# Adding the seven Strassen sums to the residual in separate steps, and one output-gate group of 512 columns instead of two of 256

## The chip, the cores and the metric

The kernel runs on 1 core of one Trainium2 chip. The metric is the device time of one execution in microseconds (us). A core has a matrix engine, TensorE (PE in the profile, its weight loads PEld), a vector engine, VectorE (DVE), a scalar engine, ScalarE (ACT), GpSimd (POOL) and SyncE (SP), which here issues the weight transfers. Each engine works through its own list of instructions in order and waits on the others by semaphores.

## The reference

Two encoder layers on `x` of 256 tokens by 2048 channels in float32. The first layer mixes tokens by pooling and attention, the second by a bidirectional matrix memory (mLSTM) with 8 heads of 256. After each mixer comes a gated MLP with a width-3 convolution. Cut to what the change touches:

```
# second layer's mixer, after the scans gave h_fw + h_bw
o_gate = sigmoid(proj[..., 3*W:4*W])
hn = hsum * rsqrt(mean(hsum*hsum) + eps) * h_norm      # per head
y = (hn * o_gate) @ w_out
# gated MLP (both layers), D_FF = 5632
u = conv3(rms_norm(x) @ w_up) ; gate, val = split(u)
x = x + (silu(gate) * val) @ w_down
```

## The kernel before, in words

**Matmuls in three terms.** Every float32 product is computed as high times high, high times low and low times high part. A weight chunk (128 x 1024) is loaded by SyncE (L100), ACT casts it to its high part (L120), DVE subtracts that to get the low part (L121): "a split". `Stream` (L79) keeps loads five and splits two chunks ahead; four split buffers `hl` rotate, so a cast waits until PE has finished the chunk four before.

**Woven tasks.** `Weave` (L145) holds generators. After each k tile of a matmul group, `tick` lets virtual time advance and runs at most one task that is due; so small pieces of work are placed between matmuls. PE's order is as written. The orders of ACT, DVE and SP are set by a scheduler that plays the program through on a modelled timeline, except where `keep_in_program_order` fixes an instruction.

**The MLP** (`ffn_layer`, L911). The 44 tiles of the inner width come in chunks of 4, 8, 8, 8, 8, 8 (`FCH`). For each tile, `up` (L929) runs 64 + 64 matmuls, then a chain on DVE and ACT: gather (L400, L401), scale (L933), convolution (L938 to L942), SiLU (L946), product (L947), high part of `g` (L948, ACT), low part (L949, DVE). The output's left 1024 columns are computed by `down` (L1043) chunk by chunk. The right 1024 columns of the first five chunks are computed with seven products instead of eight (Strassen in Winograd's form): `unit` (L973) runs products and adds them chunk by chunk into `acc`, seven tiles of 128x512 (L998, L1000). When the fifth chunk's products are complete, `total` (L1004) adds the sums of `acc` to `x`: two operations within `acc` (L1008, L1009) and nine on `x` (L1013). It is called while the last tile's chain is still on the way; then the sixth and last chunk goes through `down` for all four 512-column blocks `b`, as tiles `dn` (in the second layer the last block as `end`, L1015). `residual` (L407, adding at L410) adds a finished block to `x`. In the first layer, `nxt.add(b)` then squares the block and weaves in its transposes (`xt`, L288), whose results are scaled into `xx` (L300, L303) for the next layer.

**The mixer of the second layer** (`mlstm_layer`, L701) handles head pairs `hp` = 0 to 3: values `mv`, queries and keys `mq` and `mk`, and output gates `mo`. `mov_group` (L375) runs a group with the activations as stationary operand: 6 matmuls per k tile, of `width` columns. For `hp` 0 to 2 the pair's gates are one group of 512 columns, for the last pair two groups of 256 (L899 to L903). `gated` (L848) then takes exp (L851), adds one (L855), takes reciprocals in place (L857), multiplies the head (L861), transposes it (`htr`, L866) and writes it to `mcat` (L870, L871). `out_proj` (L412) first multiplies heads 0 to 5 for blocks 0 and 1, waits by `ready` for heads 6 and 7, and goes on with them.

The order of the weights on the host (`_ml_chunks`, L1111) follows that of the groups.

Of the kernel before, what the change touches and what calls it, by code (L numbers as in the profile page):

```python
# [190 lines left out]
def trunk(ctx: ExitStack, tc: tile.TileContext, gx, xT, xn, call, catt, cml, weights, out):  # L191
# [167 lines left out]
    def mov_part(ps, act, kts, first, last):  # L359

        n = len(kts)
        hl = None
        for i, k in enumerate(kts):
            if i % 2 == 0:
                hl = st.next()
            src, c = act(k), i % 2 * 512
            wh, wl = hl[:, 0, c : c + 512], hl[:, 1, c : c + 512]
            for t in range(2):
                xh, xl = (src[:, j, t * P : t * P + P] for j in range(2))
                mm(ps[:, t], xh, wh, first and i == 0, False)  # L370
                mm(ps[:, t], xh, wl, False, False)
                mm(ps[:, t], xl, wh, False, last and i == n - 1)
            wv.tick(1.29)
# [33 lines left out]
    def residual(ps, b, eng=None):  # L407
        for t in range(2):
            xs = x[:, t, b * 512 : b * 512 + 512]
            v.tensor_add(xs, xs, ps[:, t])  # L410
# [290 lines left out]
    def mlstm_layer(norm, nxt):  # L701
        with ExitStack() as es:
# [145 lines left out]
            def gated(ps, heads):  # L848
                og = t1p.tile([P, 2, len(heads) * MD], F32, tag="og", name=f"og{heads[0]}")
                for t in range(2):  # L850
                    a.activation(og[:, t, :], ps[:, t, :], AF.Exp, scale=nrcol[:, t : t + 1])  # L851
                yield 1.2
                for i, h in enumerate(heads):
                    o = og[:, :, i * MD : i * MD + MD]
                    v.tensor_scalar_add(o, o, 1.0)  # L855
                    for t in range(2):
                        tc.keep_in_program_order(v.reciprocal(o[:, t], o[:, t]))  # L857
                        yield 2.5
                    yield from wv.wait(lambda: h in hns)
                    hn = hns[h]  # L860
                    tc.keep_in_program_order(v.tensor_mul(hn, hn, o))  # L861
                    yield 4.5
                    tr = psp.tile([P, 2, S], F32, tag="ps", name=f"htr{h}")
                    for e in range(2):
                        for t in range(2):
                            pe.transpose(tr[:, e, t * P : t * P + P], hn[:, t, e * P : e * P + P], ident)  # L866
                    for e in range(2):
                        c = cat(2 * h + e)
                        gn = cst[:, C_HN + 2 * h + e : C_HN + 2 * h + e + 1]
                        a.activation(c[:, 0, :], tr[:, e, :], AF.Copy, scale=gn)  # L870
                        v.scalar_tensor_tensor(c[:, 1, :], tr[:, e, :], gn, c[:, 0, :].bitcast(F32),  # L871
                                               ALU.mult, ALU.subtract)
                    done.add(h)
# [3 lines left out]
            for hp in range(MH // 2):  # L877
                vf = t1p.tile([P, 2, 512], F32, tag="vf", name=f"mvf{hp}")
                for c, n in ((0, MD + 32), (MD, MD)) if hp == 0 else ((0, 512),):
                    ps = mov_group(xx, f"mv{hp}_{c}", n)  # L880
                    if hp + c == 0:
                        wv.until(lambda: norm.rcol is not None)
                        wv.add(gates(ps))
                    n = min(n, 512 if hp else MD)
                    for t in range(2):
                        a.activation(vf[:, t, c : c + n], ps[:, t, :n], AF.Copy, scale=norm.rcol[:, t : t + 1])
                vt = t1p.tile([P, 2, 2, 512], F32R, tag="vt", name=f"mvt{hp}")
                a.copy(vt[:, 0], vf)
                v.tensor_sub(vt[:, 1], vf, vt[:, 0].bitcast(F32))
                if hp == 0:  # L890
                    nrcol = kp.tile([P, 2], F32, tag="nrcol", name="nrcol")
                    v.tensor_scalar_mul(nrcol, norm.rcol, -1.0)
                for hh in range(2):
                    h = 2 * hp + hh
                    q = scaled(stat_group(xx, list(range(KT)), f"mq{h}"), f"q{h}", MD ** -0.5)
                    kk = scaled(stat_group(xx, list(range(KT)), f"mk{h}"), f"k{h}", 1.0)
                    wv.add(head(h, q, kk, vt, hh))
                heads = [2 * hp, 2 * hp + 1]
                if hp < MH // 2 - 1:  # L899
                    wv.add(gated(mov_group(xx, f"mo{hp}"), heads))  # L900
                else:
                    for h in heads:
                        wv.add(gated(mov_group(xx, f"mo{hp}_{h}", MD), [h]))  # L903

            def ready(i):
                wv.until(lambda: set(range(6 + 2 * i)) <= done)
# [4 lines left out]
    def ffn_layer(layer, norm, nxt):  # L911
        with ExitStack() as es:
# [60 lines left out]
            def unit(kind, c, j):  # L973

                n = FCH[c] // 2
                order = (4, 6, 5, 3) if kind == "A" else (0, 1, 2)
                if j == 0:
                    for e in order:
                        pss[e] = psp.tile([P, 512], F32, tag="ps", name=f"pp{layer}_{c}_{e}")
                gt = gts[c]  # L980
                s3, s1 = combos[c, j]

                def part(k, t):
                    return [gt[:, 2 * j + k, i, t * P : t * P + P] for i in range(2)]

                if kind == "A":
                    xs = [[s3[:, i, m] for i in range(2)] for m in (1, 0, 2)] + [part(1, 1)]
                else:
                    xs = [part(0, 0), part(1, 0), [s1[:, i] for i in range(2)]]
                for m, e in enumerate(order):  # L990
                    if m % 2 == 0:
                        hl = st.next()
                    wh, wl = (hl[:, i, m % 2 * 512 : m % 2 * 512 + 512] for i in range(2))
                    product(pss[e], xs[m], wh, wl, j == 0, j == n - 1)
                if j == n - 1:
                    for e in order:
                        if c == 0:
                            a.copy(acc[:, e], pss[e])  # L998
                        else:
                            v.tensor_add(acc[:, e], acc[:, e], pss[e])  # L1000
                    if kind == "B" and c == len(FCH) - 2:
                        total()

            def total():  # L1004

                p1, p2, p3, q4, p5, q6, p7 = (acc[:, e] for e in range(7))
                x00, x01, x10, x11 = (x[:, t, c : c + 512] for t in range(2) for c in (1024, 1536))
                v.tensor_sub(q6, q6, p1)  # L1008
                v.tensor_sub(p5, q6, p5)  # L1009
                for xs, op, e in ((x01, v.tensor_add, p5), (x01, v.tensor_sub, p3), (x11, v.tensor_add, p5),  # L1010
                                  (x11, v.tensor_sub, p7), (x10, v.tensor_sub, q6), (x10, v.tensor_add, p7),
                                  (x10, v.tensor_add, q4), (x00, v.tensor_add, p1), (x00, v.tensor_add, p2)):
                    op(xs, xs, e)  # L1013

            def down_end(gt, b, kts):  # L1015

# [26 lines left out]
            def down(c, b):  # L1043
                gt, last = gts[c], c == len(FCH) - 1
                kts = list(range(FCH[c]))
                if last and nxt is None and b == NB - 1:
                    down_end(gt, b, kts)
                    return
                ps = mmp.tile([P, 2, 512], F32, tag="mm", name=f"dn{layer}_{c}_{b}")
                mov_part(ps, lambda k: gt[:, k], kts, True, True)  # L1050
                residual(ps, b)
                if last and nxt is None:
                    nc.sync.dma_start(out[:, :, b * 512 : b * 512 + 512], x[:, :, b * 512 : b * 512 + 512])
                elif last:
                    nxt.add(b)
# [55 lines left out]
def _ml_chunks(w_in, w_out):  # L1111
    a = []
    for hp in range(MH // 2):
        c = 2 * D + hp * 512
        a.append(_mov(w_in[:, c : c + 512]) if hp else _stat(w_in[:, c + MD : c + 512], range(KT)))
        for h in (2 * hp, 2 * hp + 1):
            for part in (0, 1):
                c = part * D + h * MD
                a.append(_stat(w_in[:, c : c + 256], range(KT)))
        wo = w_in[:, 3 * D + hp * 512 : 3 * D + hp * 512 + 512]  # L1120
        a += [_mov(wo)] if hp < MH // 2 - 1 else [_stat(wo[:, :MD], range(KT)), _stat(wo[:, MD:], range(KT))]
    return np.concatenate(a), _out_chunks(w_out, ML_PARTS)


# [162 lines left out]
```

## Time and profile before

| | |
|---|---|
| median of 3 runs | 2203.77 us (2203.28 to 2204.05) |
| profiled execution, time | 2203.67 us |
| profiled execution, span | 2201.9 us |
| mean granted PE clock | 0.995 |
| PE / PEld busy | 2181.5 / 1871.5 us |
| DVE / ACT busy | 1669.3 / 1374.3 us |
| DMA, mean | 210 GB/s |

The span runs from the first to the last instruction; the time has a little before and behind it (1.8 us here). A busy engine is busy by its records; matmuls are pipelined, so the spacing of matmuls, not their length, says how fast PE works. An idle time is given with its releaser, the instruction that ended it. Only idle time of the engine that bounds the kernel costs time.

### The profile page before, as it was taken

What the parts mean: (1) busy time and instruction counts of PE and PEld (TensorE: products, weight loads), DVE (VectorE), ACT (ScalarE), POOL (GpSimd) and SP (SyncE); (2) the same over time, 40 slices, a digit from 0 to 9 for tenths busy, and PEclk for the clock granted to TensorE, in tenths of its full rate; (3) what the DMA queues carried; (4) which work ended last, traced back from release to release, by engine and by line L of the source; (5) the groups of instructions that cost most, each with busy time, mean ns of one, the idle gap of its engine ahead of it and who ended that gap; (6) DMA issues with size and microseconds to landing.
All of it is one profiled execution on the core that took longest, in us unless ns stands there. A gap on an engine that the chain in (4) does not pass through costs nothing.

```text
span 2201.9 us, 31410 instructions
## 1 busy us (share of the span) xinstructions
PE 2181.5 (99%) x11604; PEld 1871.5 (85%) x11604; DVE 1669.3 (76%) x2358; ACT 1374.3 (62%) x2176; POOL 59.2 (3%) x76
## 2 busy tenths in 40 slices
PE   9999999999999999989999999999999999999997
PEld 8888888888888888879888889888888888888886
DVE  7686687887878788776767677658788787888775
ACT  7665577766666676646555454557776666667662
POOL 0020000000000000000000000000000000000000
PEclk9999999999999999999999999999999999999998
DMA  9556566686867776657566555756768686777663
GB/s 324 178 164 208 175 207 228 208 244 212 260 211 248 232 229 214 206 161 203 164 197 177 186 180 167 224 179 201 231 206 245 209 258 219 239 237 232 210 210 124
DMA packets 133596, 462.97 MB, mean 210 GB/s; under 512 B 14810, under 2 KB 17154, under 8 KB 133442
## 3 DMA queue, kind: packets, MB, share of 16 engines
q1 hardware_dynamic: 125024, 438.08, 60.2%
q0 software_dynamic: 5344, 19.14, 5.1%
q10 hardware_dynamic: 3074, 3.75, 0.8%
q8 instruction: 91, 1.49, 0.3%
q14 instruction: 63, 0.52, 0.1%
HBM read 458.76 MB, written 2.14 MB: 209 GB/s over the span
## 4 chain that ended last, share of the span: by engine, by line
PE 98%; DVE 1%; issue 0%; ACT 0%; DVEq 0%
PE up L237 45%; PE dn L237 12%; PE op L237 8%; PE pp L237 8%; PE mv L237 4%; PE mq L237 4%; PE mk L237 4%; PE mo L237 4%; PE qproj L237 3%; PE pool L237 1%; PE kproj L237 1%; PE vproj L237 1%; DVE hl L121 1%; PE qk L237 1%; PE av L237 1%; PE end L237 0%
## 5 line engine op out<-in xcount | busy, mean ns | idle before, releaser
L121 DVE TENSOR_TENSOR hl<-w,hl 128x1024 fp32r<-128x1024 f32 (+2 forms) x808 | 951.8, 1193 | 263.9 <-ACT hl L120 261.6
L120 ACT CAST hl<-w 128x1024 fp32r<-128x1024 f32 (+2 forms) x807 | 817.3, 1028 | 458.7 <-PE up L237 138.7
L237 PE MATMUL up<-xx,hl 128*128 128x512 f32 (+1 forms) x5632 | 993.6, 337 | 0.0
L237 PEld LDWEIGHTS up<-xx,hl 128*128 128x128 f32 x5632 | 867.0, 188 | 130.4
L237 PE MATMUL dn<-hl,g 128*128 128x512 f32 x1200 | 282.7, 395 | 15.2 <-ACT g L948 15.2
L237 PEld LDWEIGHTS dn<-hl,g 128*128 128x128 f32 x1200 | 228.1, 191 | 64.1 <-ACT g L948 16.1
L400 ACT COPY tb_up<-up 128x512 f32<-128x512 f32 x88 | 51.7, 587 | 134.4 <-PE up L237 134.4
L237 PE MATMUL pp<-hl,s 128*128 128x512 f32 x432 | 111.2, 393 | 0.0
L940 ACT ACTIVATE y<-tb_up,cst 128x256 f32<-128x256 f32 x176 | 103.9, 590 | 0.0
L401 DVE TENSOR_TENSOR tb_up<-up,tb_up 128x512 f32<-128x512 f32 x88 | 60.7, 690 | 55.2 <-ACT tb_up L400 55.2
L941 DVE TENSOR_TENSOR y<-y,z 128x510 f32<-128x510 f32 x88 | 60.6, 689 | 52.4 <-ACT y L940 51.8
L938 ACT ACTIVATE z<-tb_up,cst 128x256 f32<-128x256 f32 x176 | 88.6, 503 | 12.6 <-DVE tb_up L933 12.3
L237 PE MATMUL mk<-xx,hl 128*128 128x512 f32 (+1 forms) x512 | 92.2, 337 | 0.0
L237 PE MATMUL mq<-xx,hl 128*128 128x512 f32 (+1 forms) x512 | 92.1, 337 | 0.0
L237 PE MATMUL mv<-hl,xx 128*128 128x512 f32 (+2 forms) x480 | 91.7, 350 | 0.0
L237 PE MATMUL mo<-hl,xx 128*128 128x512 f32 (+1 forms) x480 | 91.6, 348 | 0.0
L237 PE MATMUL op<-hl,cat 128*128 128x512 f32 x384 | 91.6, 393 | 0.0
L237 PEld LDWEIGHTS pp<-hl,s 128*128 128x128 f32 x432 | 78.5, 188 | 15.1
L237 PE MATMUL op<-hl,mcat 128*128 128x512 f32 x384 | 89.5, 392 | 0.0
L237 PEld LDWEIGHTS mq<-xx,hl 128*128 128x128 f32 x512 | 79.2, 188 | 11.6
L237 PEld LDWEIGHTS mk<-xx,hl 128*128 128x128 f32 x512 | 79.0, 188 | 11.4
L237 PEld LDWEIGHTS mv<-hl,xx 128*128 128x128 f32 x480 | 78.3, 189 | 11.2
(230 smaller groups left out, 1992.5 us busy)
## 6 DMA issues: line engine op xcount, KB each, us to landing
w<-in_up SPq DMA_DIRECT2D x352, 512.0 KB, 4.3
w<-in_dn SPq DMA_DIRECT2D x176, 512.0 KB, 4.5
w<-in_m_in SPq DMA_DIRECT2D x124, 512.0 KB, 4.1
w<-in_a_in SPq DMA_DIRECT2D x46, 512.0 KB, 4.5
sum<-in_dn SPq DMA_DIRECT2D x36, 512.0 KB, 4.7
sum<-in_dn POOLq DMA_DIRECT2D x36, 512.0 KB, 7.6
w<-in_a_out SPq DMA_DIRECT2D x32, 512.0 KB, 3.5
w<-in_m_out SPq DMA_DIRECT2D x32, 512.0 KB, 4.2
```

Source lines behind the costliest of these rows:

```text
L120: (self.nc.vector.tensor_copy if i + c == 0 else self.nc.scalar.copy)(hl[:, 0, c : c + n], w[:, c : c + n])
L121: self.nc.vector.tensor_sub(hl[:, 1, c : c + n], w[:, c : c + n], hl[:, 0, c : c + n].bitcast(F32))
L237: pe.matmul(out_, lhsT, rhs, start=start, stop=stop, skip_group_check=True)
L400: a.copy(tb, ps[:, :, 1, :])
L401: v.tensor_add(tb, ps[:, :, 0, :], tb)
L938: a.activation(z[:, 0, j, :], u[:, j, :], AF.Copy, scale=cw(tl, 0))
L940: a.activation(y[:, j, :], u[:, j, :], AF.Identity, scale=cw(tl, 1), bias=cw(tl, 3))
L941: v.tensor_add(y[:, :, 1:S], y[:, :, 1:S], z[:, 0, :, 0 : S - 1])
```

## The change

In both MLPs, `total` becomes a generator. It goes to the woven tasks with a virtual delay of 12 us, and each of its eleven operations is one step, 1.3 virtual us apart. The order of the steps is another: first all that ends in the third 512-column block (`x10`, `x00`), then the fourth (`x01`, `x11`). Each step is fixed in program order. The difference `q6 - p5` takes the place of `p5 = q6 - p5` and is formed in `q6`. Before the residual of blocks 2 and 3 of the last chunk, the weave is run until the steps are all issued.

In the mixer, the last pair's gates become one group of 512 columns with one `gated` task for both heads, and the weight chunks on the host follow.

```
--- before.py
+++ after.py
@@ -895,12 +895,7 @@
                     wv.add(head(h, q, kk, vt, hh))
-                heads = [2 * hp, 2 * hp + 1]
-                if hp < MH // 2 - 1:
-                    wv.add(gated(mov_group(xx, f"mo{hp}"), heads))
-                else:
-                    for h in heads:
-                        wv.add(gated(mov_group(xx, f"mo{hp}_{h}", MD), [h]))
+                wv.add(gated(mov_group(xx, f"mo{hp}"), [2 * hp, 2 * hp + 1]))
@@ -999,18 +994,20 @@
                     if kind == "B" and c == len(FCH) - 2:
-                        total()
+                        wv.add(total(), 12.0)
 
             def total():
 
                 p1, p2, p3, q4, p5, q6, p7 = (acc[:, e] for e in range(7))
                 x00, x01, x10, x11 = (x[:, t, c : c + 512] for t in range(2) for c in (1024, 1536))
-                v.tensor_sub(q6, q6, p1)
-                v.tensor_sub(p5, q6, p5)
-                for xs, op, e in ((x01, v.tensor_add, p5), (x01, v.tensor_sub, p3), (x11, v.tensor_add, p5),
-                                  (x11, v.tensor_sub, p7), (x10, v.tensor_sub, q6), (x10, v.tensor_add, p7),
-                                  (x10, v.tensor_add, q4), (x00, v.tensor_add, p1), (x00, v.tensor_add, p2)):
-                    op(xs, xs, e)
+                steps = [(q6, v.tensor_sub, p1), (x10, v.tensor_sub, q6), (x10, v.tensor_add, p7),
+                         (x10, v.tensor_add, q4), (x00, v.tensor_add, p1), (x00, v.tensor_add, p2),
+                         (q6, v.tensor_sub, p5), (x01, v.tensor_add, q6), (x01, v.tensor_sub, p3),
+                         (x11, v.tensor_add, q6), (x11, v.tensor_sub, p7)]
+                for to, op, e in steps:
+                    tc.keep_in_program_order(op(to, to, e))
+                    yield 1.3
+                pss["total"] = True
@@ -1048,6 +1045,8 @@
                 mov_part(ps, lambda k: gt[:, k], kts, True, True)
+                if last and b >= 2:
+                    wv.until(lambda: "total" in pss)
                 residual(ps, b)
@@ -1118,7 +1117,7 @@
         wo = w_in[:, 3 * D + hp * 512 : 3 * D + hp * 512 + 512]
-        a += [_mov(wo)] if hp < MH // 2 - 1 else [_stat(wo[:, :MD], range(KT)), _stat(wo[:, MD:], range(KT))]
+        a.append(_mov(wo))
```

## The prediction

> **What bounds the kernel now.** I read the page first (engine shares, chain), then the list of waits of TensorE, then the timeline around the one wait that is left.
>
> ```profile
> span 2201.9 us, 31410 instructions
> PE 2181.5 (99%) x11604; PEld 1871.5 (85%) x11604; DVE 1669.3 (76%) x2358; ACT 1374.3 (62%) x2176; POOL 59.2 (3%) x76
> PE 98%; DVE 1%; issue 0%; ACT 0%; DVEq 0%
> ```
>
> TensorE (PE) has work in 2181.5 of 2201.9 us and is 98% of the chain. So only two things can save time: a gap in PE that closes, or matmuls that take less. The waits of PE and of its weight loads say where the gaps are (us in total, times, longest):
>
> ```profile
> PE dn L237 <- ACT g L948: 15.2, 2, 7.6
> PEld dn L237 <- DVE g L949: 0.2, 1, 0.2
> ```
>
> Both stand at one place: the last K chunk of the down projection, once per layer, waiting for the last gated tile `g`. The timeline of the second layer (start, length, engine, line, operation; in brackets the idle time and who ended it):
>
> ```profile
> 2144.07 9.68 PE L237 MATMUL dn<-hl,g 128*128 128x512 f32 x42
> 2146.37 0.68 DVE L1000 TENSOR_TENSOR acc<-acc,pp 128x512 f32<-128x512 f32 x1
> 2146.97 0.68 DVE L1008 TENSOR_TENSOR acc<-acc 128x512 f32<-128x512 f32 x1
> 2148.14 1.05 ACT L120 CAST hl<-w 128x1024 fp32r<-128x1024 f32 x1
> 2148.17 2.36 DVE L121 TENSOR_TENSOR hl<-w,hl 128x1024 fp32r<-128x1024 f32 x2
> 2149.71 1.06 ACT L120 CAST hl<-w 128x1024 fp32r<-128x1024 f32 x1 [0.52 <-PE dn L237]
> 2150.44 0.68 DVE L1009 TENSOR_TENSOR acc<-acc 128x512 f32<-128x512 f32 x1
> 2152.43 1.06 ACT L120 CAST hl<-w 128x1024 fp32r<-128x1024 f32 x1 [1.66 <-PE dn L237]
> 2156.93 0.68 DVE L942 TENSOR_TENSOR y<-y,z 128x510 f32<-128x510 f32 x1
> 2157.70 0.42 ACT L946 ACTIVATE s<-y 128x256 f32<-128x256 f32 x1 [4.22 <-DVE y L942]
> 2160.47 0.41 DVE L947 TENSOR_TENSOR s<-s,y 128x256 f32<-128x256 f32 x1
> 2160.92 0.41 ACT L948 CAST g<-s 128x256 fp32r<-128x256 f32 x1 [2.80 <-DVE s L947]
> 2161.35 0.43 DVE L949 TENSOR_TENSOR g<-s,g 128x256 fp32r<-128x256 f32 x1 [0.47 <-ACT g L948]
> 2161.38 25.72 PE L237 MATMUL dn<-hl,g 128*128 128x512 f32 x102 [7.62 <-ACT g L948]
> ```
>
> PE runs seven of the eight k tiles and stops at 2153.76. The eighth needs `g`, whose chain (L941, L942, L946 to L949) stands on VectorE (DVE) mixed with the eleven operations of `total()`; nine of these per layer are in one group of the view by lines (count, then busy us and mean ns), beside the group of weight loads needed below:
>
> ```profile
> L1013 DVE TENSOR_TENSOR x<-x,acc 128x512 f32<-128x512 f32 x18 | 11.6, 682 | 0.0
> L237 PEld LDWEIGHTS dn<-hl,g 128*128 128x128 f32 x1200 | 228.1, 191 | 64.1 <-ACT g L948 16.1 <-DVE g L949 0.2
> ```
>
> The gap costs more than its 7.62 us. Windows around both gaps (length, five busy times with counts for PE, PEld, DVE, ACT, POOL, then PEclk, the granted clock):
>
> ```profile
> 941.70:944.30 2.60, 0.00 (x0) 0.00 (x0) 2.60 (x5) 0.00 (x0) 0.00 (x0) 1.00 0.66 183
> 944.40:949.30 4.90, 0.00 (x0) 0.00 (x0) 4.90 (x9) 0.82 (x2) 0.00 (x0) 0.50 0.65 245
> 2153.80:2156.00 2.20, 0.00 (x0) 0.00 (x0) 2.20 (x4) 0.00 (x0) 0.00 (x0) 1.00 0.35 97
> 2156.20:2161.30 5.10, 0.00 (x0) 0.00 (x0) 4.68 (x8) 0.80 (x2) 0.00 (x0) 0.50 0.67 247
> 2161.40:2166.30 4.90, 4.90 (x12) 3.84 (x13) 2.34 (x4) 1.04 (x1) 0.00 (x0) 0.50 0.03 9
> 2166.40:2169.00 2.60, 2.60 (x13) 2.15 (x12) 0.36 (x1) 0.86 (x1) 0.00 (x0) 1.00 0.83 249
> ```
>
> Some 2.3 to 2.7 us after PE stops its clock falls to 0.50, and it stays there for about 5 us after PE has work again: 12 matmuls in 4.90 us, then 13 in 2.60. The chain prices that:
>
> ```profile
> 2080.58 10.88 PE dn L237 x48
> 949.31 8.23 PE dn L237 x24
> ```
>
> Undisturbed, a 512-column matmul takes 10.88/48 = 0.2267 us. After the first layer's gap 24 took 8.23 instead of 5.44, a loss of 2.8 us; after the second layer's, 102 took 25.72 instead of 23.12, a loss of 2.6 us. So the ends lose 7.62 + 2.8 = 10.4 and 7.62 + 2.6 = 10.2 us, **20.6 us** together. That is the most this part can return.
>
> **The change, part one: the sums step by step.** The same eleven 128x512 operations remain; their order and place change. In the built changed kernel DVE's list at both ends runs: L1000, two splits (L121), L941, split, L942, split, L947, split, the first of the sums, L949; the other ten stand behind the residuals of the first output block. ScalarE's (ACT) list has the third cast (L120) after L946 instead of before. I lay this order out with the rows above. Pitches: one split 1.135 (two of them from 2148.17 to 2150.44), a 128x512 operation 0.60 (2146.37 to 2146.97).
>
> - The two splits start at 2146.97 and 2148.11, L941 at 2149.24, a split at 2149.84 (its cast ended at 2149.19), L942 at 2150.98, a split at 2151.58 (cast ended 2150.77), free at 2152.71.
> - L946 follows L942's start by 0.77 (2156.93 to 2157.70): 2151.75 to 2152.17. L947 starts at 2152.71.
> - L948 could start 0.45 after L947 (2160.47 to 2160.92), at 2153.16, but ACT holds the third cast, which waits for PE until 2152.43, to 2153.49. So L948 starts at about 2153.4, and PE follows 0.46 later (2160.92 to 2161.38): 2153.86, against 2153.76. This wait is 0.1 us.
> - The third matmul of that k tile reads the low half, L949. Ahead of it on DVE stand the split of the third cast (2153.5, when that cast ends) and the first sum (2154.65), so L949 runs from 2155.25 to 2155.67. PE would have been there at 2153.76 + 2 x 0.227 = 2154.21 and gets there at 2155.7 to 2155.9, after a weight load of up to 0.19. **The end now loses 1.6 us** (1.5 to 1.7).
>
> The first layer has the same instructions, so it loses the same. Returned: 10.4 - 1.6 = 8.8 and 10.2 - 1.6 = 8.6, together **17.4 us**, if the clock stays at 1.00. The trace has no idle time between 0.2 and 7.62 us behind dense matmuls, so it does not show what 1.5 us idle does. Bounds: nothing, or one relapse (below). I take nothing, as the clock stood at 1.00 for more than 2.2 us of idling.
>
> The Trainium skill, "TensorE: Matmul & The Clock Gate", section "What's actually happening", says the clock is halved by default and after at least one idle window of about 3.4 us, and is restored after one busy window of that length. By the Trainium skill 1.5 us is safe. The trace partly disagrees: the drop came after 2.3 to 2.7 us, so a window need not be wholly idle, and the relapse stays among the rivals.
>
> The ten steps that move behind the gap lie beside PE's remaining blocks. What covers them, in the first layer, which is the denser (residuals, transposes, normalisation):
>
> ```profile
> 949.30:988.60 39.30, 39.29 (x174) 32.20 (x175) 23.93 (x33) 21.30 (x36) 0.00 (x0) 0.93 0.46 135
> 965.31 1.28 DVE L410 TENSOR_TENSOR x<-x,dn 128x512 f32<-128x512 f32 x2 [0.41 <-PE dn L237]
> 969.19 0.60 PE L288 MATMUL xt<-cst,x 128*128 128x128 f32 x4
> ```
>
> DVE is busy 23.93 of 39.30 us there; ten steps of 0.68 make 30.7, and without the 2.8 us of slow clock the stage is 36.5 long: 84%, still beside PE. The tightest link is a residual (L410) ahead of the transposes (L288) that read it: 969.19 less 966.59 leaves 2.6 us. In the new order two steps stand ahead of that residual, which with the split before it makes it about 1.6 us late; 1 us of slack is left. Cost: 0. If the cover failed, PE would wait by the excess at up to six transposes.
>
> **Part two: one group of 512 columns.** Two groups of 96 matmuls of 256 columns become one of 96 of 512. The chain has both forms, with the same foreign matmuls between:
>
> ```profile
> 1254.95 8.17 PE mo L237 x36
> 1280.13 13.60 PE mv L237 x60
> 1350.73 7.19 PE mo L237 x60
> 1377.08 2.75 PE op L237 x12
> ```
>
> The third pair (one group) takes 1280.13 - 1254.95 = 25.18 us, the last (two groups) 1377.08 - 1350.73 = 26.35. **Saved: 1.2 us.** The Trainium skill, "TensorE: Matmul & The Clock Gate", section "Back-to-back issue gap", gives an isolated spacing of N/2.4 + 2.5 ns; by it (an estimate) 192 x 109.2 less 96 x 215.8 ns is 0.25 us, and the sum would end 0.9 us higher. It also says that real spacing differs because weight loads share the stream. The rows decide.
>
> Both heads' gates now start only when the group ends. The built order of DVE, ACT and PE then equals that of the third pair, with the reciprocals ahead of splits, so its rows are the model:
>
> ```profile
> 1282.00 0.76 DVE L855 TENSOR_SCALAR og<-og 128x512 f32<-128x512 f32 x2 [2.12 <-ACT og L851]
> 1292.03 0.69 DVE L861 TENSOR_TENSOR hn<-hn,og 128x512 f32<-128x512 f32 x1
> 1293.57 0.60 PE L866 MATMUL htr<-cst,hn 128*128 128x128 f32 x4
> ```
>
> The product L861 ends at 1292.72, the transposes start at 1293.57 after 60 matmuls without waiting: 0.85 us to spare, and the changed kernel also has 60 matmuls ahead of them. The second head's transposes stand 48 matmuls later, in the output projection's second block; the columns they feed are read 144 matmuls (32.7 us) after the projection starts, some 4 us after they are ready. Two prefetches (L105) move behind three weight loads on SyncE's queue; the sums they load are used in the FFN that follows. Cost of all this: 0.
>
> **The sum.** 17.4 + 1.2 = 18.6 us. The profiled execution took 2203.67 us, 0.10 under the median; 2203.77 - 18.6 = **2185.2 us**.
>
> **The rivals.**
>
> - *The clock relapses.* If 1.5 us idle suffices in one clock window, the half clock would last about one further window. From the rows: it lasted from 2156.1 to 2166.35, 10.2 us, and PE had work only in the last 5.0 of them; a full third of the 10.2, 3.4 us, at half speed loses about 1.7 us per end. Time: 2187 (one end) to 2188.6 (both). For it: the drop came with less than 3.4 us idle. Against: it never came in the first 2.2 us. Chance 0.13.
> - *The gap stays larger.* If a cast, a split or a weight transfer in my layout is late (three casts wait for a buffer that PE frees), every 1 us delays `g` by 1 us in both layers, and from some 2.5 us on the clock falls as well: 2190 to 2198. Against: DVE's and ACT's lists are fixed, and every row used is of the same instructions. Chance 0.07.
> - *It does not do what it says*: the steps stay ahead of `g`. Then only part two is left, 2202.6. One of eleven does stay, priced above. Chance 0.02.
> - *DVE becomes the bound behind the gap (slower).* A chunk of 12 matmuls lasts 2.72 us; DVE has about 2.3 us of work in it with the steps (84%). In my layout the third split ends at 2154.6 and PE reaches its chunk at 2162, so splits run some 7 us ahead; if DVE needed over 2.72 us per chunk that lead would go, and PE would wait at each of the 12 chunks behind each gap, 24 in all. To end above 2208.2 it takes 23 us, 0.96 per chunk, so DVE work of 3.7 us per chunk (less if the waits grew past 2.3 us and halved the clock). Only contention that makes DVE's work 1.6 times as long could do it; no row shows that. Chance 0.04.
>
> **How the numbers follow.** The forecast has 0.74: all 20.6 us of the ends back plus 1.2 would be 2182; both ends a little worse with no gain from part two, 2187. The range takes 2182.5 to 2189, which adds the relapse and leaves out the rest. A measurement of this kernel can tell about 0.2% (4.4 us) from no change: faster 0.94 (forecast, relapse, larger gap), same 0.02, slower 0.04.
>
> **What the profile after would show.** Right: the wait of `dn` for L948 falls from 15.2 us to about 0.2, one for L949 grows to some 1.3 per layer; PEclk stays 1.00 in both windows, and 48 matmuls of the second block take 10.9 us; the steps of the sums stand behind L949; the last `mo` group takes about 25.2 us. Wrong: PEclk of 0.50 after the ends, waits of L288 for L410, or of `htr` for L861, or of `dn` for a split.

## The result, and the profile after

| | before | changed |
|---|---|---|
| median, measured side by side, 6 runs each | 2203.55 us (2202.84 to 2204.05) | 2185.92 us (2185.60 to 2186.63) |
| profiled execution, time | 2203.67 us | 2185.79 us |
| profiled execution, span | 2201.9 us | 2184.0 us |
| mean granted PE clock | 0.995 | 1.000 |

The ratio is 0.9921, interval 0.9908 to 0.9933: 17.6 us less. In the changed kernel the line numbers behind L898 are 5 lower (L948 is L943, L949 is L944), and all sums stand at L1008. The page of the changed kernel, its head and engines:

```profile
span 2184.0 us, 31216 instructions
...
PE 2176.3 (100%) x11508; PEld 1862.4 (85%) x11508; DVE 1668.1 (76%) x2358; ACT 1373.8 (63%) x2174; POOL 59.3 (3%) x76
```

PE has 96 matmuls less (part two), DVE the same 2358 operations as before. The waits of PE and of its weight loads (us in total, times, longest):

```profile
PE dn L237 <- DVE g L944: 2.3, 2, 1.2
...
PEld dn L237 <- DVE g L944: 3.2, 2, 1.6
...
PEld dn L237 <- ACT g L943: 1.0, 2, 0.5
```

The wait for the high part of `g`, 15.2 us before, is gone from PE's list; what is left on it is a wait for the low part at each end. The weight loads also wait 0.5 us for the high part at each end. The timeline of the second layer's end:

```profile
2134.30 9.48 PEld L237 LDWEIGHTS dn<-hl,g 128*128 128x128 f32 x42
2134.53 10.50 PE L237 MATMUL dn<-hl,g 128*128 128x512 f32 x44
...
2140.17 1.06 ACT L120 CAST hl<-w 128x1024 fp32r<-128x1024 f32 x1 [0.53 <-PE dn L237]
2140.30 1.22 DVE L121 TENSOR_TENSOR hl<-w,hl 128x1024 fp32r<-128x1024 f32 x1
2141.43 0.68 DVE L937 TENSOR_TENSOR y<-y,z 128x510 f32<-128x510 f32 x1
...
2142.89 1.06 ACT L120 CAST hl<-w 128x1024 fp32r<-128x1024 f32 x1 [0.26 <-PE dn L237]
2143.17 0.42 DVE L942 TENSOR_TENSOR s<-s,y 128x256 f32<-128x256 f32 x1
2143.84 0.40 ACT L943 CAST g<-s 128x256 fp32r<-128x256 f32 x1
2143.98 1.23 DVE L121 TENSOR_TENSOR hl<-w,hl 128x1024 fp32r<-128x1024 f32 x1 [0.39 <-ACT hl L120]
2144.29 0.30 PEld L237 LDWEIGHTS dn<-hl,g 128*128 128x128 f32 x2 [0.51 <-ACT g L943]
2145.12 0.69 DVE L1008 TENSOR_TENSOR acc<-acc 128x512 f32<-128x512 f32 x1
2145.72 0.42 DVE L944 TENSOR_TENSOR g<-s,g 128x256 fp32r<-128x256 f32 x1
...
2146.19 23.00 PE L237 MATMUL dn<-hl,g 128*128 128x512 f32 x100 [1.16 <-DVE g L944]
```

Read it from the last row back. PE waited 1.16 us for L944. That operation had its input, L943, at 2144.24, but DVE worked on the third chunk's split and the first of the sums until then. The split could not start before its cast, and the cast (2142.89) stands ahead of L943 on ACT, as laid out. The granted clock around both ends (length, busy us and count of PE, PEld, DVE, ACT, POOL, then the clock):

```profile
942.00:946.00 4.00, 2.84 (x11) 2.04 (x12) 2.71 (x5) 0.92 (x1) 0.00 (x0) 1.00 0.92 266
946.00:950.00 4.00, 4.00 (x21) 3.33 (x20) 2.60 (x3) 2.92 (x7) 0.00 (x0) 1.00 0.57 214
2144.00:2147.00 3.00, 1.75 (x6) 0.97 (x6) 2.14 (x3) 0.24 (x1) 0.00 (x0) 1.00 0.89 320
2147.00:2150.00 3.00, 3.00 (x15) 2.44 (x14) 2.56 (x4) 1.05 (x1) 0.00 (x0) 1.00 0.49 180
```

It stays at 1.00. The chain, around the last gates:

```profile
1342.39 8.17 PE mo L237 x36
...
1367.57 13.60 PE op L237 x60
1381.17 0.44 PE htr L866 x4
```

The last pair now takes 1367.57 - 1342.39 = 25.18 us, and `htr` follows the 60 matmuls without a wait. Where the time went, by the first matmul of each stage in PE's timeline:

| stage, us | before | changed | difference |
|---|---|---|---|
| start to the first layer's last chunk (`dn`) | 932.00 | 932.18 | +0.18 |
| that chunk, to `mv` | 56.81 | 48.28 | -8.53 |
| `mv` to the last pair's `mo` | 361.76 | 361.77 | +0.01 |
| last `mo`, to `op` | 26.35 | 25.18 | -1.17 |
| `op` to the second layer's last chunk | 767.15 | 767.12 | -0.03 |
| three blocks of that chunk, to `end` | 42.86 | 34.50 | -8.36 |

Three stages hold the whole gain, and nothing is given back elsewhere. 144 undisturbed matmuls take 32.65 us, so the second end still loses 34.50 - 32.65 = 1.85 us. The starts of single matmuls in PE's timeline show where: the last one ahead of `g`, the two that read its high part, and the first two from its low part on.

```profile
2143.82 0.39 PE L237 MATMUL dn<-hl,g 128*128 128x512 f32 x1
2144.30 0.50 PE L237 MATMUL dn<-hl,g 128*128 128x512 f32 x1
2144.63 0.40 PE L237 MATMUL dn<-hl,g 128*128 128x512 f32 x1
2146.19 0.50 PE L237 MATMUL dn<-hl,g 128*128 128x512 f32 x1 [1.16 <-DVE g L944]
2146.53 0.40 PE L237 MATMUL dn<-hl,g 128*128 128x512 f32 x1
```

Undisturbed, one starts every 0.227 us. The first that needs the high part is 2144.30 - 2143.82 - 0.23 = 0.25 us late, the first that needs the low part 2146.19 - 2144.63 - 0.23 = 1.33. Behind each of the two waits the next start comes after 0.34 us, and behind the second wait some ten more follow at 0.23 to 0.24 before the spacing is 0.227 again: 0.27 us in all. These three make up the 1.85 us.

### The profile page after: what moved, and what is told of

Its sections match the earlier page's. It is cut to its first block, busy times and chain, and to the rows that moved or that the text cites. A ratio compares the mean times of both kernels' runs of the same rounds, so it can differ in the third digit from the quotient of the medians.

```text
span 2184.0 us, 31216 instructions
## 1 busy us (share of the span) xinstructions
PE 2176.3 (100%) x11508; PEld 1862.4 (85%) x11508; DVE 1668.1 (76%) x2358; ACT 1373.8 (63%) x2174; POOL 59.3 (3%) x76
## 4 chain that ended last, share of the span: by engine, by line
PE 99%; DVE 0%; ACT 0%; issue 0%
PE up L237 45%; PE dn L237 12%; PE op L237 8%; PE pp L237 8%; PE mv L237 4%; PE mq L237 4%; PE mk L237 4%; PE mo L237 4%; PE qproj L237 3%; PE kproj L237 1%; PE pool L237 1%; PE vproj L237 1%; PE qk L237 1%; PE av L237 1%; PE end L237 0%; PE xt L288 0%
## 5 line engine op out<-in xcount | busy, mean ns | idle before, releaser
L237 PE MATMUL mo<-hl,xx 128*128 128x512 f32 x384 | 90.4, 391 | 0.0
```

What stands on the lines that cost most here:

```text
L237: pe.matmul(out_, lhsT, rhs, start=start, stop=stop, skip_group_check=True)
```

## The experiments

**Theory**: each end lost time because `g` stood behind the sums on DVE, in two parts, the wait itself and the half clock that it brings; with the sums out of the way only the wait for the low part is left, and DVE hides the other ten steps. **Rivals**: the remaining wait is long enough to bring the half clock in some executions; DVE becomes the bound behind the gap; part two, not the sums, gives some of the gain at the ends. All kernels were run with repeated timing, each beside runs of the kernel before on the same chip. The stages of their profiles, as above:

| stage | e1_sums | e2_gates | e3_busy | e4_pin | e5_lag2 | e8_lag3 | e6_lag4 | e7_double | e9_after | e10_pin |
|---|---|---|---|---|---|---|---|---|---|---|
| start to `dn` | 932.29 | 933.08 | 932.08 | 932.07 | 932.38 | 932.40 | 934.48 | 933.61 | 932.42 | 932.63 |
| `dn` to `mv` | 48.30 | 56.34 | 54.54 | 46.61 | 49.01 | 51.33 | 52.07 | 48.89 | 48.28 | 46.62 |
| `mo` to `op` | 26.34 | 25.18 | 26.34 | 25.18 | 25.18 | 25.18 | 25.18 | 25.18 | 25.18 | 25.18 |
| `op` to `dn` | 767.32 | 767.13 | 769.61 | 767.91 | 767.12 | 767.12 | 768.35 | 767.13 | 767.21 | 768.57 |
| `dn` to `end` | 34.49 | 43.19 | 40.56 | 32.81 | 36.79 | 37.41 | 38.27 | 36.71 | 34.46 | 32.81 |

**e1_sums: part one alone.** The changed kernel with the gates as before:

```
-                wv.add(gated(mov_group(xx, f"mo{hp}"), [2 * hp, 2 * hp + 1]))
+                heads = [2 * hp, 2 * hp + 1]
...
+                        wv.add(gated(mov_group(xx, f"mo{hp}_{h}", MD), [h]))
```

> Only part one: the sums go step by step, the last pair's gates stay two groups of 256 columns. Theory (the gap at the ends of both MLPs and the half clock behind it made nearly all of the gain): the loss of the two ends falls as in the changed kernel, by 16.9 us (8.5 and 8.4 between the traces), so 2203.55 - 16.9 = 2186.7 us, 1.2 slower than the changed kernel within a few tenths. Rival (the gate group brings more than its own 1.2 us, for instance by moving what follows): 2188 or more.

Measured: 2188.07 us (2187.24 to 2188.59), ratio 0.9927 (0.9915 to 0.9939).

```profile
PE dn L237 <- DVE g L949: 2.3, 2, 1.2
```

Both ends and the wait are those of the changed kernel to 0.02 us; only the gates' stage is back at 26.34. So the gain at the ends is part one's. The time itself lies where the rival put it (2188 or more): 15.9 us below the kernel before on this chip (2204.01 us), where 16.9 were expected. The profiled execution (2187.24 us) rules the rival out, since its gates' stage is 1.16 us longer than that of the changed kernel and no more; what the other executions lost beside it is not known.

**e2_gates: part two alone.** The kernel before with one group:

```
-                heads = [2 * hp, 2 * hp + 1]
...
+                wv.add(gated(mov_group(xx, f"mo{hp}"), [2 * hp, 2 * hp + 1]))
```

> Only part two: one gate group of 512 columns, the sums as before. Theory: the group lasts 25.18 instead of 26.35 us and nothing else moves: 2203.55 - 1.2 = 2202.4 us. Rival (gates that start later make the output projection wait, so that the two parts do not add up): 2203.5 or more.

Measured: 2203.16 us (2202.21 to 2203.92), ratio 0.9995 (0.9986 to 1.0004).

```profile
PE dn L237 <- ACT g L943: 15.2, 2, 7.6
```

The old wait is there whole, and the gates' stage is 25.18. By the time alone part two cannot be told from nothing; by its stage it saves 1.17 us.

**e3_busy: the half clock by itself.** The kernel before, with 30 matmuls into a tile that nobody reads, put ahead of the last k tile so that PE works through most of the gap:

```
+            if fill and i == n - 1:
+                busy = psp.tile([P, 512], F32, tag="ps", name="busy")
+                for j in range(fill):
+                    mm(busy, act(0)[:, 0, 0:P], hl[:, 0, 0:512], j == 0, j == fill - 1)
```

> The kernel before, with 30 matmuls of 512 columns ahead of the last k tile of the first output block of each MLP's last chunk; nothing reads their result. They fill about 6.8 of the 7.62 us in which PE waits for g, so PE still goes on at the same moment, but it has worked. Theory (the gap costs 7.62 us and, apart from that, 2.8 and 2.6 us of half clock): the clock stays at 1.00, the gap itself stays, 2203.55 - 5.4 = 2198.1 us. Rival (the slow matmuls behind the gap are not due to its idling): no gain, 2203.5 us, and PEclk of 0.50 as before.

Measured: 2200.40 us (2199.50 to 2202.93), ratio 0.9985 (0.9976 to 0.9994), mean clock 1.000. PE's timeline at the second end:

```profile
2153.85 6.96 PE L237 MATMUL busy<-hl,g 128*128 128x512 f32 x30
2161.63 6.65 PE L237 MATMUL dn<-hl,g 128*128 128x512 f32 x28 [0.82 <-ACT g L952]
```

`g` is as late as before, but no clock is lost, and the ends are 2.27 and 2.30 us shorter. So the half clock is a price of its own, 2.3 us in the profiled execution of the kernel before, and not 2.8 and 2.6. It differs between executions: e2_gates has the same two waits of 7.62 us, its half clock lasted 6.8 us at the first end and 10.2 at the second (10.2 at both in the kernel before), and its ends are 56.34 - 54.54 = 1.80 and 43.19 - 40.56 = 2.63 us longer than those of e3_busy. The second end still loses 40.56 - 32.65 = 7.91 us to the wait alone, 0.29 more than the 7.62 of idle time that PE's records show; the prediction had put that to the clock. About half of it is how records count: this row (shortest, median and longest matmul in ns), from the view of the tile `dn` in the changed kernel, says that one is recorded with 389 ns, where one starts every 227, so an idle time by records is some 0.16 us short.

```profile
L237 PE MATMUL dn<-hl,g x1200: 387/389/504, 315.8 to 2168.8; 128*128 128x512 f32 x172
```

The other half, some 0.15 us, is the slower spacing of the first matmuls behind a wait, here 0.34 and then 0.23 to 0.24 us, with the clock at 1.00. The time fell by less than the ends did, 3.6 us against 4.6. In the profiled run the stage before the second end is 2.5 us longer than in the kernel before, and PE waited there once for a split, 1.7 us in `pp`.

**e4_pin: the rest of the wait.** The changed kernel, with order-only dependencies that put the third chunk's cast behind L943 on ACT, and that chunk's split and the first of the sums behind L944 on DVE:

```
+            if i == self.hold:
+                self.behind(hi, self.g[0])
+                self.behind(lo, self.g[1])
...
+                    if i == 0:
+                        st.behind(step, st.g[1])
```

> The changed kernel, with three instructions held behind g at each end: the third cast behind the high part of g on ACT, its low part and the first sum behind the low part of g on DVE. Theory (what is left of the gap is the wait for g, 0.5 and 1.2 us by PE's list of waits, 1.85 us by the spacing of matmuls): high and low part of g are there 0.2 and 1.3 us earlier, the loss per end falls from 1.85 to 0.3 us or less, 2185.92 - 3.2 = 2182.7 us. Rival (the rest of the gap is fixed by the chain L941 to L949 itself, or the delayed split makes PE wait later): 2185 to 2186 us.

Measured: 2183.24 us (2182.67 to 2184.22), ratio 0.9906 (0.9893 to 0.9920). Its timeline at the second end:

```profile
2142.62 0.41 ACT L952 CAST g<-s 128x256 fp32r<-128x256 f32 x1 [0.99 <-DVE s L951]
2142.93 1.04 ACT L121 CAST hl<-w 128x1024 fp32r<-128x1024 f32 x1
2143.06 0.42 DVE L953 TENSOR_TENSOR g<-s,g 128x256 fp32r<-128x256 f32 x1 [0.47 <-ACT g L952]
...
2143.53 14.60 PEld L246 LDWEIGHTS dn<-hl,g 128*128 128x128 f32 x65 [0.16 <-DVE g L953]
2144.01 1.23 DVE L122 TENSOR_TENSOR hl<-w,hl 128x1024 fp32r<-128x1024 f32 x1 [0.53 <-ACT hl L121]
```

The low part now follows the high part at once, the ends are 46.61 and 32.81, and PE's list has no wait for `g` any more; 32.81 - 32.65 = 0.16 us is left, the slower spacing of the first matmuls that read `g`. What still cost time at the ends of the changed kernel was indeed the cast, the split and the one step ahead of L944.

**e5_lag2, e8_lag3, e6_lag4: a longer wait.** The changed kernel with 2, 3 or 4 extra operations of 128x512 on DVE ahead of L944, to find the wait at which the clock falls. One of them runs in a moment in which DVE was idle, so PE's wait grows by less than their length:

```
...
+                for _ in range(2 if end else 0):
+                    tc.keep_in_program_order(v.tensor_mul(u, u, u))
```

> The changed kernel with 2 more DVE operations of 128x512 (nothing reads their result) between the product and the low part of the last g at each end, 0.7 us each, of which some 0.4 fit into an idle moment of DVE. PE's wait for the low part grows from 1.2 to about 2.1 us. Theory (the clock only falls after some 2.3 us or more without work): only the delay is paid, 1.0 per end, 2187.9 us, PEclk 1.00. Rival (the relapse: less idling suffices where it falls into one clock window): 1.7 to 2.3 us more per end that relapses, up to 2192.

> As before this one, with 3 more DVE operations per end: PE's wait is about 2.8 us. Only the delay: 2189.3 us. With a relapse at one or both ends: 2191 to 2194. The trace of the kernel before had the drop 2.3 and 2.7 us after PE stopped, so here I expect it at least at one end.

> As before, with 4 more DVE operations per end: PE's wait is about 3.5 us. Only the delay: 2190.7 us. With a relapse at both ends, which I expect here: 2194 to 2195.5, and PEclk of 0.50 behind both ends for 3 to 5 us.

Measured: 2190.34 us (2188.99 to 2192.15), ratio 0.9939 (0.9926 to 0.9953); 2191.78 (2190.10 to 2194.59), 0.9946 (0.9933 to 0.9960); 2196.47 (2194.04 to 2197.29), 0.9965 (0.9951 to 0.9978). PE's longest wait is 1.9, 2.6 and 3.3 us. The clock fell at one end of e5_lag2 and at both ends of the two others, each time for 3.41 us. This holds for the profiled executions; the four runs of e5_lag2 had mean clocks from 0.998 to 1.000, which suggests that the number of drops differs between executions. In the profiled one of e5_lag2 the first end grew by 0.73 us, the wait alone; the second by 2.29, so the half clock cost 1.56. The changes of the clock within one execution lie on a grid of 3.413 us (in the kernel before the two drops are 355 steps of it apart), so I cut the windows on that grid. e5_lag2 (PE's busy time is the second number behind the window):

```profile
943.17:946.58 3.41, 1.81 (x8) 1.51 (x9) 2.12 (x5) 0.58 (x1) 0.00 (x0) 1.00 0.80 270
...
2144.66:2148.07 3.41, 1.44 (x6) 0.58 (x5) 3.13 (x5) 0.51 (x2) 0.00 (x0) 1.00 0.91 310
2148.07:2151.48 3.41, 3.41 (x9) 2.66 (x9) 1.70 (x3) 1.04 (x1) 0.00 (x0) 0.50 0.39 149
```

The same wait of 1.9 us straddled two windows at the first end; the window with most of it still had 1.81 us of work, and the clock stayed. At the second it fell in one window, with 1.44 us of work, and the next window ran at half clock. e8_lag3 and the kernel before agree: windows at whose end the clock fell.

```profile
942.38:945.79 3.41, 0.80 (x3) 0.36 (x3) 3.04 (x5) 0.00 (x0) 0.00 (x0) 1.00 0.87 314
...
2147.28:2150.70 3.42, 0.93 (x3) 0.30 (x2) 3.38 (x6) 0.23 (x1) 0.00 (x0) 1.00 0.81 262
```

```profile
940.97:944.38 3.41, 0.71 (x4) 0.25 (x2) 3.41 (x5) 0.45 (x1) 0.00 (x0) 1.00 0.71 209
2152.70:2156.11 3.41, 1.05 (x5) 0.55 (x3) 3.41 (x5) 0.78 (x1) 0.00 (x0) 1.00 0.49 168
```

**e7_double: is DVE the bound?** The changed kernel with a second operation of the same size behind each step of the sums, into a tile that nobody reads:

```
...
                     tc.keep_in_program_order(op(to, to, e))
+                    tc.keep_in_program_order(v.tensor_mul(spare, e, e))
```

> The changed kernel with a second 128x512 DVE operation behind each step of the sums (nothing reads its result). The first of them stands ahead of g and costs its 0.6 us at each end. Theory (the steps behind the gap lie beside PE, with DVE at 84% of the stage and splits running 7 us ahead): the other ten cost nothing or, in the first layer, where DVE comes to about 100%, up to 1 us: 2187.1 to 2188 us. Rival (DVE is already the bound behind the gap, so that each operation there shows): 10 x 0.6 = 6 us more in the first layer and as much in the second, 2195 to 2199.

Measured: 2190.03 us (2188.45 to 2191.63), ratio 0.9938 (0.9925 to 0.9952). Behind the first gap DVE was busy 29.07 of 34.50 us in the changed kernel, and is busy 32.84 here:

```profile
951.20:985.70 34.50, 34.50 (x180) 29.38 (x180) 29.07 (x48) 20.60 (x35) 0.72 (x1) 1.00 0.53 159
```

```profile
951.20:985.70 34.50, 34.50 (x175) 29.06 (x174) 32.84 (x50) 19.29 (x32) 0.00 (x0) 1.00 0.48 154
```

PE has no idle time in either. The first end grew by 0.61 us, which is the one extra operation ahead of L944; the other ten cost nothing, even with DVE at 95% of these 34.5 us. The second end grew by 2.21, as the wait brought the half clock there. Its windows at the first and the second end:

```profile
941.82:945.23 3.41, 2.21 (x9) 1.19 (x7) 3.02 (x5) 1.36 (x2) 0.00 (x0) 1.00 0.92 317
...
2146.71:2150.12 3.41, 1.65 (x8) 1.06 (x7) 2.13 (x5) 0.05 (x1) 0.00 (x0) 1.00 0.91 341
2150.12:2153.54 3.42, 3.42 (x10) 2.65 (x9) 3.42 (x5) 0.99 (x1) 0.00 (x0) 0.50 0.36 143
```

**e9_after and e10_pin: the changed and the pinned kernel on one chip.** No further edit.

> The changed kernel once more, beside the pinned one on the same chip. Both theories (wait for the low part is all that is left; or it also carries a chance of a clock loss): 2185.6 to 2186.7 us with the granted clock at 1.00 at both ends, stages 48.3 and 34.5. If the remaining idle time at the seams sometimes meets the clock's window badly, single runs of this kernel lie 1.6 us higher (2187.2 to 2188.3), and the pinned kernel's don't.

> The pinned kernel again, directly against the changed one: by the stages of its first run (46.61 and 32.81 against 48.28 and 34.50) 3.4 us below it, 2182.3 to 2183.3 us. If the first run's gain was the chip's and not the order's: within 1 us of the changed kernel.

Measured: 2186.30 us (2185.67 to 2187.06, 5 runs), ratio 0.9918 (0.9905 to 0.9932), and 2183.75 (2182.66 to 2184.31, 4 runs), ratio 0.9905 (0.9892 to 0.9919). The pinned kernel is 2.55 us faster and the ranges do not meet, so it beats both kernels. Its ends gain 1.66 and 1.65 us, 3.3 together, as expected; part of that was lost elsewhere: in the profiled run the stage from `op` to the second layer's last chunk is 1.36 us longer than in e9_after, and the weight loads of `up` waited 1.9 us for splits there. Behind one of these waits stands a late weight transfer:

```profile
2003.34 0.69 DVE L117 TENSOR_TENSOR w<-w,sum 128x512 f32<-128x512 f32 x1 [2.17 <-DMA w<-in_dn]
```

Such waits stand in e3_busy, e6_lag4 and e7_double too, which have no pins. Whether the pins make them more frequent was not tried. All 11 runs of the changed kernel had a mean clock of 1.000.

## Why the prediction was right, point by point

- **The bound and the price of the ends: right.** Taken from the pinned kernel's ends (46.61 and 32.81, each with 0.16 left), the kernel before lost 10.36 and 10.21 us, against 10.4 and 10.2. The two parts were cut at the wrong place, which leaves their sum as it is: the last matmul ahead of the second gap starts at 2153.36, so the next could have started at 2153.59 and the wait is 7.79 us, not 7.62; the slow stretch lost that much less. That the half clock is a separate part of it is shown by e3_busy, at 2.3 us per end in these executions and 1.80 and 2.63 in that of e2_gates.
- **The layout of the new order: right to 0.05 us.** The last chunk starts 9.54 us earlier than before; with that added, L943 starts at 2153.38 (forecast 2153.4), L944 at 2155.26 (2155.25), and the load behind it at 2155.73 (2155.7 to 2155.9).
- **The loss that stays, 1.6 us per end: mis-sized, 1.85.** The instructions came where they were expected, and so did the matmul that waits for the low part, at 2155.73. Two things in this term were wrong. The forecast took the end of the last matmul's record, 2153.76, for the moment at which PE could go on; by the starts it is 2153.59, so the matmul on the low part would have started at 2154.04 and is 1.69 us late, not 1.52 (and the wait for the high part is 0.25 us, not 0.1). And it had nothing for the slower spacing behind that wait, 0.16 us. Together these give the 1.85. So 16.9 us came back at the ends instead of 17.4.
- **The ten steps at no cost: right**, shown by e7_double with twice the steps. The share of DVE was forecast a little too high: from the end of the wait to `mv`, the stage that the forecast used, DVE is busy 29.07 of 36.40 us, 80% and not 84, and 32.13 of 36.40 with twice the steps. The forecast counted 0.68 us for a step, the length of its record, where steps in a dense list follow each other after 0.60. The rival of DVE as the bound falls.
- **Part two, 1.2 us: right** (1.17), with no wait of `htr`. The isolated spacing by the formula of the Trainium skill, "TensorE: Matmul & The Clock Gate", section "Back-to-back issue gap", would have given an estimated 0.25; the trace does not agree.
- **No relapse: right, but the reason given was too weak.** I argued that the clock had never fallen in the first 2.2 us of idling. A shorter wait is enough: e7_double lost it with one of 1.76 us, which lay in one window as a whole. So it was not the 2.2 us that made the changed kernel safe. Its 1.16 us leaves enough work in a window, and the mean clock was 1.000 in all 11 runs. At its second end the whole wait lies in one:

```profile
2144.81:2148.22 3.41, 2.25 (x10) 1.66 (x10) 2.11 (x5) 0.78 (x1) 0.00 (x0) 1.00 0.88 305
```

  2.25 us of work (2.16 at the same place in e9_after), where the clock stayed with 1.70 and more in every profiled execution. The price of a relapse of one window was right: 1.7 forecast, 1.56 measured in e5_lag2.
- **A larger gap, or steps that stay ahead of `g`: no.** Every cast and split came at its forecast place, and the first of the eleven is the only step ahead of L944.
- **The sum.** 16.9 + 1.2 = 18.1 us by stages, less some 0.2 in stages that the change doesn't touch: 17.9 between the profiled executions, 17.6 between the medians, against 18.6. The small miss is the term of the remaining loss, twice 0.25, the 0.2 that lies outside the change, and 0.2 by which the median of the kernel before is lower here than in its first three runs (2203.55 against 2203.77).

## What to carry to other kernels

When a chain of small operations feeds the matrix engine, look at what else stands on its engines' lists ahead of each link; work that nobody waits for yet belongs behind the last link, and one cast, one split and one step of the sums left ahead of it cost 1.7 us at each end here, more than the whole second part of the change gave. Price a gap of the matrix engine as its wait plus the half clock that it may bring, and take the second from windows of the trace, not from the length of the wait alone. A change of one microsecond is proved by the length of its stage, where the time of the whole kernel can't tell it from nothing.

## What the runs showed of the hardware that was not expected

The granted clock changes on a grid of 3.413 us that runs through an execution. In the profiled executions it fell from 1.00 to 0.50 at the end of every window in which PE was busy for 1.44 us or less by its records, and stayed at the end of every one with 1.70 us or more. Between these the records do not decide: it fell with 1.65 us (e7_double) and stayed with 1.55, in the window of e10_pin's last matmuls. The lowest of the windows behind which it stayed, in e10_pin and, at the first end, in e2_gates:

```profile
2177.06:2180.47 3.41, 1.55 (x7) 0.94 (x5) 1.38 (x2) 0.00 (x0) 0.00 (x0) 1.00 0.27 107
```

```profile
941.07:944.48 3.41, 1.70 (x8) 1.08 (x6) 3.41 (x5) 1.05 (x1) 0.00 (x0) 1.00 0.58 175
```

So about half a window of idling decides. By the Trainium skill, "TensorE: Matmul & The Clock Gate", section "What's actually happening", the clock is halved after at least one idle window of about 3.4 us; the length of the window agrees, that it must be idle throughout does not. The clock came back at the end of a window in which PE was busy for 3.20 us or more, and not of one with 2.25 us or less. In the kernel before, which had one idle and one partly busy window behind the drop, it took three windows, 10.2 us; in e2_gates the first drop came one window later against the same wait, and it took two. Because the grid does not start with the kernel's work, the same wait of 1.8 or 1.9 us cost 1.6 us of half clock at one end of an execution and nothing beside itself at the other.
